# Stick-breaking heads: q and k projected with stationary weights, a GpSimd product for the second chunk, and idle projection tiles lent as extra buffers

## The chip, the core and the metric

The kernel runs as one program on one core of a Trainium2 chip. The core has a matrix engine (TensorE, PE in the profile; its weight loads are the row PEld), a vector engine (VectorE, DVE), a scalar engine (ScalarE, ACT), a general-purpose engine (GpSimd, POOL), a queue engine (SyncE, SP) that issues most of the transfers, and 16 DMA engines that carry them out. Each engine works through its own queue in order and waits on semaphores for the others. The metric is the device time of one execution in microseconds, lower is better. Numbers that are compared are medians of several executions; the profile is of one execution.

## The reference

The reference is one layer of a residual block over 2048 positions of width 1024, in float32. What matters here is the stick-breaking half of the attention:

```python
u = rms_norm(x, norm1_w)
proj = u @ w_in                       # -> diff q, k, v | sb q, sk, sv
# 4 differential-attention heads on the first half, then 8 stick-breaking heads of width 64:
z = einsum('bqhd,bkhd->bhqk', qb, k) * 64 ** -0.5
mask = k_pos < q_pos
log_1mb = where(mask, log_sigmoid(-z), 0)
rem = cumsum(log_1mb, reverse=True) - log_1mb
a = where(mask, exp(log_sigmoid(z) + rem), 0)
out = einsum('bhqk,bkhd->bqhd', a, v)
# then: h = x + concat(y_diff, rms_norm(y_sb)) @ w_out ; h = h + SwiGLU(rms_norm(h))
```

For each query row, every earlier key gets a weight beta = sigmoid(z) times the product of (1 - beta) over the keys between it and the query. The kernel forms that product directly with a scan over sigmoid(-z), from the last key to the first.

## The kernel before

Almost every matrix product is taken in split float16: a float32 number is held as a high half and a low half, and a product is the sum of three float16 products (high by high, high by low, low by high) accumulated in PSUM. So most tensors exist as a pair of halves, and "split" in the code means making that pair.

The attention runs over eight groups g. Groups 0 to 3 are the four differential heads; groups 4 to 7 are two stick-breaking heads each (index m = 0, 1 within the group). For each group there is a projection (`proj`, 16 row tiles t of 128 positions) and an attention part (`diff_attn` for g < 4, `sb_attn` for the others). The projections run ahead of the attention: `advance` emits tiles of group g + 1 while group g attends, so matrix work of the projection lies among the attention's. The order in each engine's queue is set by a scheduler when the program is built, from the order of emission, the priorities in `PRI` and its own model of times; `note` and `pick` keep a running account of the load of ACT, DVE and POOL, and choose an engine for operations that may go to more than one.

A projection tile before (`proj_tile`, line 320) loads a 128 by 128 piece of the normalised input as the stationary operand and streams 384 columns of the weights past it (128 for q, 128 for k, 128 for v): 24 matmuls of 384 columns for one tile, into one PSUM tile `pj`. There are two such PSUM tiles (`psj`, two buffers). `proj_out` then splits v, and for g >= 4 splits q and k into the staging tile `st` (lines 327 and 330). Positions lie on the partitions there, but the scores need the head dimension on the partitions, so after every four tiles `proj_batch` turns `st` with two transposing transfers into `qT` and `kT` (line 372), and two more transfers copy the halves of `qT` with their partition halves exchanged (line 374). In `kT` each head m has its 64 high rows and its 64 low rows stacked on the 128 partitions; with `qT` stacked the same way and with the exchanged copy, two matmuls give all four products of halves.

One step of `sb_attn` is `stage_a(i, m, b)`: query tile i, head m, key block b of up to 1024 keys, done in chunks of up to 512 keys, from the last chunk (c = 1 where the block has more than 512 keys) to the first (c = 0). For a chunk, `score_chunk` (line 448) puts scores into one of four PSUM tiles `sc`; ACT writes sigmoid(-z) into the SBUF tile `om` (line 554) and sigmoid(z) over the scores in PSUM (line 555); DVE runs the reversed product scan over `om` (line 557) and multiplies the two into `be` (line 558). Where a query tile has two key blocks, the first column of one block's `om` is copied to the next (line 547). When the block is whole, `split_t` makes the high half of `be` on ACT (line 89) and the low half on POOL (line 98) in a tile `s16` (three buffers), and one transposing transfer, issued by SP, turns both into `aT` (line 403, six buffers). `stage_b` multiplies `aT` with v (`pv`, line 458). Up to PD = 5 steps wait between the two stages. The tiles `z4` for `be` and `om` have nine buffers.

Group 7 has no projection after it; instead the output projection of the finished rows (`out_proj`, line 761) is placed beside it. The projection's pool (`pp`) also holds the tiles `st` and `raw`, two buffers each. `raw` is used by the projections of g < 4, and `st` by all; in group 7 `raw` takes a part of the output weights and `st` the residual rows. After the attention comes the SwiGLU part, which the change does not touch.

Of the kernel before, what the change touches and what calls it, by code (L numbers as in the profile page):

```python
# [11 lines left out]
F32 = mybir.dt.float32  # L12
# [18 lines left out]
NG = 8  # L31
# [28 lines left out]
def block(tc, a, out):  # L60
# [3 lines left out]
    with top:  # L64
# [62 lines left out]
        DVE.memset(mhalf[:], -0.5)  # L127

# [122 lines left out]
        with ExitStack() as ph1:  # L251
# [71 lines left out]

            def split_psum(hi, lo, src, n):
# [8 lines left out]
            @pri("po")  # L333
            def proj_out(g, G, pj, B, j):
                st, v, raw = B
                nv = 1 if g < 4 else 2
                vv = v[:, j, :].rearrange("p (h s e) -> p h s e", h=nv, s=2)
                split_psum(vv[:, :, 0, :], vv[:, :, 1, :], pj[:, 256:384].rearrange("p (h e) -> p h e", h=nv), 128)
                if g < 4:
                    if pick(A=270, D=335) == "A":  # L340
                        ACT.mul(raw[:, j, :], pj[:, :256], 2.0 ** -11)
                    else:
                        DVE.tensor_scalar(raw[:, j, :], pj[:, :256], 2.0 ** -11, None, op0=ALU.mult)
                else:
                    split_psum(st[:, 0:4, j, 0, :], st[:, 0:4, j, 1, :], pj[:, :256].rearrange("p (c e) -> p c e", c=4), 256)

            @pri("pb")
            def proj_batch(g, G, B):
                st, v, raw = B
                qT = sp.tile([P, 4, 4, P], F16, tag="qT", bufs=QB, name=nm("qT"))  # L350
                kT = sp.tile([P, 2, 4, P], F16, tag="kT", bufs=KB, name=nm("kT"))
                if g < 4:
                    rq = raw[:].rearrange("p t (c e) -> p t c e", e=64)
                    sq = st[:].rearrange("p c t s e -> p (c t s e)")[:, :2048].bitcast(F32)
                    ACT.activation(sq.rearrange("p (t c e) -> p t c e", t=4, c=4), rq, AF.Square)
                    note("A", 950)
                    ss = sm.tile([P, 16], F32, tag="ss", bufs=2, name=nm("ss"))
                    DVE.tensor_reduce(ss[:], sq.rearrange("p (c e) -> p c e", e=64), op=ALU.add, axis=AX.X)
                    rs = sm.tile([P, 16], F32, tag="rs", bufs=2, name=nm("rs"))
                    rstd(rs[:], ss[:], 2.0 ** -16 / 64, G["epsk"][:])  # L360
                    rsb = rs[:].rearrange("p (t c) -> p t c", c=4).unsqueeze(3).to_broadcast([P, 4, 4, 64])
                    DVE.tensor_tensor(rq, rq, rsb, ALU.mult)
                    note("D", 2300)
                    gb = gk[:].unsqueeze(1).unsqueeze(1).to_broadcast([P, 4, 2, 64])
                    tt(rq[:, :, 2:4, :], rq[:, :, 2:4, :], gb, ALU.mult, 512)
                    for o in range(2):
                        src = rq[:, :, 2 * o : 2 * o + 2, :]
                        d = st[:, 2 * o : 2 * o + 2].rearrange("p c t s e -> p t c s e")
                        to16(d[:, :, :, 0, :], src, 512)
                        tt(d[:, :, :, 1, :], src, d[:, :, :, 0, :], ALU.subtract, 512)  # L370
# [8 lines left out]
            def proj(g, G, fresh=None):  # L379
                for t in range(NT):  # L380
# [6 lines left out]
                    if t % 4 == 0:  # L387
                        st = pp.tile([P, 4, 4, 2, 64], F16, tag="st", name=nm("st"))
                        v = sp.tile([P, 4, 256], F16, tag="v", bufs=KB, name=nm("v"))
                        raw = pp.tile([P, 4, 256], F32, tag="raw", name=nm("raw")) if g < 4 else None  # L390
# [145 lines left out]
            def sb_attn(g, G):  # L536
# [691 lines left out]
```

## Time and profile before

| | us |
|---|---|
| median of three runs (lowest, highest) | 2735.74 (2730.43, 2737.0) |
| the profiled execution | 2740.3 |
| its span from first to last instruction | 2738.5 |
| busy in the span: PE / DVE / POOL / ACT | 2490.0 / 1978.5 / 1429.8 / 1353.3 |
| first and last start of the stick-breaking sigmoid (line 554) | 605.4 and 1378.7 |

A row of the profile's groups reads: line, engine, operation, written tile <- read tiles, shape, count, then busy time in us, mean duration in ns, and the idle time of the engine just before these instructions with what ended it. The matmul durations overlap, because matmuls are pipelined; their rate is read from the starts of consecutive runs in the timeline. The granted clock of PE is a share of full speed.

### The profile page before, as it was taken

The page shows a single profiled execution, that of the slowest core. Times are in us where ns is not written, and L with a number is a line of the kernel's source. Part 1 is how long each engine was busy: PE and PEld are TensorE (multiplying, and loading weights), DVE is VectorE, ACT ScalarE, POOL GpSimd, SP SyncE. Part 2 cuts the span into 40 slices and gives each one's busy share as a digit, 9 for nine tenths or more (in the row PEclk, how much of TensorE's full clock was granted, in tenths as well). Part 3 has the DMA queues.
Part 4 walks back from the last instruction along what each step waited for, and adds up shares of the span by engine and source line. Part 5 has one row for each costly group of instructions (what it writes and reads, how often), then busy time and mean ns, then how long its engine had stood idle before and what let it go on. Part 6 is the DMA issues. An engine that isn't in the chain of part 4 may idle for free.

```text
span 2738.5 us, 45414 instructions
## 1 busy us (share of the span) xinstructions
PE 2490.0 (91%) x17084; PEld 1409.8 (51%) x17084; DVE 1978.5 (72%) x3752; ACT 1353.3 (49%) x2539; POOL 1429.8 (52%) x1002
## 2 busy tenths in 40 slices
PE   7998989898978886889989898999999999999999
PEld 4655656565545553457775444444444444444444
DVE  6888879888888989987766777777786544434434
ACT  4665656566868778765644534344342212121121
POOL 2577677765554545546655566565664332222322
PEclk9999999998999997899999999999999999999999
DMA  6788787789998997997896665566657845635532
GB/s 227 199 164 178 151 198 164 180 171 200 208 201 184 212 186 151 203 192 208 213 289 256 220 234 191 208 221 216 231 204 283 316 158 181 220 128 193 192 116 93
DMA packets 646830, 543.52 MB, mean 198 GB/s; under 512 B 506369, under 2 KB 573953, under 8 KB 636369
## 3 DMA queue, kind: packets, MB, share of 16 engines
q1 hardware_dynamic: 644784, 538.53, 71.8%
q8 instruction: 134, 2.20, 0.3%
q0 software_dynamic: 512, 1.36, 0.2%
q10 hardware_dynamic: 1312, 0.72, 0.1%
q14 instruction: 88, 0.71, 0.1%
HBM read 261.08 MB, written 147.32 MB: 149 GB/s over the span
## 4 chain that ended last, share of the span: by engine, by line
PE 36%; DVE 9%; DMA 4%; POOL 3%; issue 3%; ACT 2%; SPq 0%; DVEq 0%; POOLq 0%; ACTq 0%
PE pd L1034 14%; PE pm L934 7%; PE pd L934 5%; PE pa L934 5%; DVE wd L215 2%; PE po L761 2%; DMA stages<-in_w_down_dram 1%; POOL stages L98 1%; DVE wu L215 1%; DMA aT<-s 1%; DVE z L557 1%; DVE cg L999 1%; DVE cg L98 1%; POOL s L98 1%; PE pj L320 1%
## 5 line engine op out<-in xcount | busy, mean ns | idle before, releaser
L98 POOL TENSOR_TENSOR s<-z,s 128x1024 f16<-128x1024 f32 (+7 forms) x288 | 474.4, 1655 | 320.1 <-ACT s L89 281.4
L320 PE MATMUL pj<-w,xt 128*128 128x384 f16 x3072 | 577.0, 336 | 19.2 <-DMA xt<-xs 5.6
L320 PEld LDWEIGHTS <-xt 128*128 128x128 f16 x3072 | 301.5, 101 | 233.1 <-issue 36.1
L557 DVE TENSOR_TENSOR_SCAN z<-z,sc 128x512 f32<-128x512 f32 (+3 forms) x320 | 356.1, 1114 | 72.1 <-ACT sc L555 68.8
L448 PE MATMUL sc<-kT,qT 128*128 128x512 f16 (+3 forms) x1280 | 348.3, 364 | 59.4 <-DVE z L558 23.7
L1034 PE MATMUL pd<-wd,act 128*128 128x512 f16 x1764 | 394.0, 381 | 7.2 <-DVE cu L968 7.1
L458 PE MATMUL yp<-v,aT 128*128 128x64 f16 (+1 forms) x4896 | 281.5, 209 | 82.3 <-DMA aT<-s 81.7
L458 PEld LDWEIGHTS <-aT 128*128 128x128 f16 x4896 | 245.4, 102 | 172.1 <-DMA aT<-s 110.4
L934 PEld LDWEIGHTS <-wg 128*128 128x128 f16 x1848 | 181.8, 98 | 228.1 <-issue 14.6
L934 PEld LDWEIGHTS <-wu 128*128 128x128 f16 x1848 | 180.8, 98 | 216.5 <-issue 2.0
L98 POOL TENSOR_TENSOR act<-cg,act 128x512 f16<-128x512 f32 x109 | 149.8, 1385 | 262.3 <-ACT act L993 262.3
L1034 PEld LDWEIGHTS <-act 128*128 128x128 f16 x1764 | 173.0, 98 | 216.6 <-issue 10.2
L89 ACT CAST s<-z 128x128 f16<-128x128 f32 (+7 forms) x216 | 170.3, 790 | 154.8 <-DMA aT<-s 72.9
L98 POOL TENSOR_TENSOR stages<-stages 128x512 f32<-128x512 f32 x97 | 172.9, 1783 | 120.1 <-DVE wg L215 41.4
L98 POOL TENSOR_TENSOR hs<-hs,cu 128x512 f32<-128x512 f32 x102 | 132.6, 1306 | 165.6 <-DVE hs L1040 62.7
L554 ACT ACTIVATE z<-sc,c 128x512 f32<-128x512 f32 (+3 forms) x320 | 204.4, 639 | 23.7 <-PE sc L448 18.9
L558 DVE TENSOR_TENSOR z<-sc,z 128x512 f32<-128x512 f32 (+3 forms) x320 | 193.7, 606 | 8.5
L555 ACT ACTIVATE sc<-sc,c 128x512 f32<-128x512 f32 (+3 forms) x320 | 196.5, 614 | 0.0
L1040 DVE SCALAR_TENSOR_TENSOR hs<-pd,c,hs 128x512 f32<-128x512 f32 x144 | 106.5, 748 | 118.5 <-PE pd L1034 113.6
L761 PE MATMUL po<-wo,mt 128*128 128x256 f16 x1536 | 180.7, 275 | 12.3 <-DVE xf L764 6.8
L993 ACT CAST act<-cg 128x512 f16<-128x512 f32 x126 | 76.9, 616 | 231.4 <-DVE cg L999 192.7
L934 PE MATMUL pm<-X,wu 128*128 128x512 f16 x792 | 179.1, 379 | 1.8 <-ACT cg L979 1.7
(241 smaller groups left out, 4109.1 us busy)
## 6 DMA issues: line engine op xcount, KB each, us to landing
xt<-xs SPq DMA_DIRECT2D x112, 512.0 KB, 4.4
hs<-hd SPq DMA_DIRECT2D x72, 512.0 KB, 4.5
hd<-hs SPq DMA_DIRECT2D x56, 512.0 KB, 5.8
split<-wg SPq DMA_DIRECT2D x11, 1792.0 KB, 6.9
split<-wu SPq DMA_DIRECT2D x11, 1792.0 KB, 6.7
split<-wd SPq DMA_DIRECT2D x11, 1792.0 KB, 6.8
wg<-split SPq DMA_DIRECT2D x11, 1792.0 KB, 7.4
wd<-split SPq DMA_DIRECT2D x11, 1792.0 KB, 9.1
```

What stands on the lines that cost most here:

```text
L89: ACT.copy(dst, src)
L98: (DVE if e == "D" else POOL).tensor_tensor(dst, a_, b_, op)
L320: PE.matmul(pj[:, :384], lhsT=xv[:, xi, kt, :], rhs=G["w"][:, wi, kt, :], start=n == 0, stop=n == 23)
L448: PE.matmul(sc[:, : 128 * w].rearrange("p (t n) -> p t n", n=P), lhsT=G["q"][i // 4][:, 2 - 2 * o + m, i % 4, :], rhs=G["k"][q][:, m, 0:w, ...
L458: PE.matmul(yp[:, y0 : y0 + wd], lhsT=aT[:, a_, :], rhs=v[:, v_ : v_ + wd], start=start and j == 0 and q == 0, stop=stop and j == nb - 1 a ...
L554: ACT.activation(om[:, lo:hi], sc[:, :w], AF.Sigmoid, scale=G["nkz"][:])
L555: ACT.activation(sc[:, :w], sc[:, :w], AF.Sigmoid, scale=G["kz"][:])
L557: DVE.tensor_tensor_scan(ov, ov, sc[:, :w], om[:, hi : hi + 1], op0=ALU.mult, op1=ALU.bypass)
L558: DVE.tensor_tensor(be[:, lo:hi], sc[:, :w], om[:, lo + 1 : hi + 1], ALU.mult)
L761: PE.matmul(po[:, sl], lhsT=mt[:, kt, P * xi : P * xi + P], rhs=wos[2 * h + n][wi][:, kt, :], start=q == 0, stop=q == 23)
L934: PE.matmul(ps_[:].rearrange("p (t n) -> p t n", n=P), lhsT=wv[:, wo, wi, 128 * kt : 128 * kt + 128], rhs=X[xo][:, :, xi, kt, :], start=st ...
L1034: PE.matmul(po[:], lhsT=act[:, ao, xi, 128 * j : 128 * j + 128], rhs=W["d"][:, wo, wi, :], start=start and u == 0 and q == 0, stop=u == nu ...
```

## The change

Four things change, all in the stick-breaking groups 4 to 7.

First, q and k are projected the other way round. `proj_turned` takes a 128 by 128 piece of the weights as the stationary operand and streams the 128 positions of the input past it, so that q and k come out with the head dimension on the partitions. Only v keeps the old orientation. A tile is now 72 matmuls of 128 columns in the place of 24 of 384. Two tiles share a pair of PSUM tiles, `pq` (q and k) and `pv` (v), which together are both buffers of `psj`. `turned_out` reads them once for the pair: q is written for each head with the other head's 64 rows multiplied by zero (the constant `half`), as a high part on ACT and a low part on DVE; k and v are split as before. The two transposing transfers and the two exchange copies for every four tiles are gone in these groups.

Second, a score chunk is three matmuls in the place of two: masked high q by high k, masked low q by high k, masked high q by low k.

Third, for the chunk c = 1 ACT writes sigmoid(z) into `be` in SBUF, and the product with the scan moves from DVE to POOL. The chunk c = 0 stays on DVE.

Fourth, in groups 4 to 6 `split_t` takes its `s16` tile from the two idle `raw` tiles in two of five steps, and its `aT` tile from the two idle `st` tiles in one of four, and 7 steps in the place of 5 may wait between the stages. Group 7 keeps the old numbers.

```diff
+        half = c1(2, "half")
+        DVE.memset(half[:], 0.0)
+        for m in range(2):
+            DVE.memset(half[64 * m : 64 * m + 64, m : m + 1], 2.0 ** -11)
...
+            @pri("pm")
+            def proj_turned(G, xt, pq, pv, r):
+                xv = xt[:].rearrange("p (s k n) -> p s k n", s=2, k=KT)
+                for c in range(3):
+                    n = 0
+                    for kt in range(KT):
+                        for xi, wi in ((0, 0), (0, 1), (1, 0)):
+                            w_, x_ = G["w"][:, wi, kt, 128 * c : 128 * c + 128], xv[:, xi, kt, :]
+                            o = pv[:, P * r : P * r + P] if c == 2 else pq[:, 256 * c + P * r : 256 * c + P * r + P]
+                            PE.matmul(o, lhsT=x_ if c == 2 else w_, rhs=w_ if c == 2 else x_, start=n == 0, stop=n == 23)
+                            n += 1
+
+            @pri("po")
+            def turned_out(pq, pv, qT, kT, v, j):
+                two = slice(j - 1, j + 1)
+                q2, k2 = (pq[:, 256 * c : 256 * c + 256].rearrange("p (t n) -> p t n", t=2) for c in range(2))
+                for m in range(2):
+                    ACT.mul(qT[:, m, two, :], q2, half[:, m : m + 1])
+                    DVE.scalar_tensor_tensor(qT[:, 2 + m, two, :], q2, half[:, m : m + 1], qT[:, m, two, :], op0=ALU.mult, op1=ALU.subtract)
+                note("A", 800)
+                note("D", 800)
+                split_psum(kT[:, 0, two, :], kT[:, 1, two, :], k2, 256)
+                vv = v[:, two, :].rearrange("p t (h s e) -> p t h s e", h=2, s=2)
+                split_psum(vv[:, :, :, 0, :], vv[:, :, :, 1, :], pv[:, :256].rearrange("p (t h e) -> p t h e", t=2, h=2), 256)
...
-                else:
-                    split_psum(st[:, 0:4, j, 0, :], st[:, 0:4, j, 1, :], pj[:, :256].rearrange("p (c e) -> p c e", c=4), 256)
...
+                    if g >= 4:
+                        if t % 4 == 0:
+                            qT, kT = new_qk()
+                            G["q"].append(qT)
+                            G["k"].append(kT)
+                            G["v"].append(v)
+                        if t % 2 == 0:
+                            pq, pv_ = (psj.tile([P, 512], F32, tag="pj", name=nm("pj")) for _ in range(2))
+                        proj_turned(G, xt, pq, pv_, t % 2)
+                        if t % 2 == 1:
+                            turned_out(pq, pv_, qT, kT, v, t % 4)
+                        yield
+                        continue
...
-            def split_t(src, n, he="ADP", le="DP"):
-                s16 = s16p.tile([P, 2048], F16, tag="s16", bufs=SB, name=nm("s16"))
+            def split_t(src, n, he="ADP", le="DP", wide=None):
+                if wide is not None and wide % 5 in (1, 3):
+                    s16 = pp.tile([P, 4, 256], F32, tag="raw", name=nm("s16"))[:].rearrange("p t n -> p (t n)").bitcast(F16)
+                else:
+                    s16 = s16p.tile([P, 2048], F16, tag="s16", bufs=SB, name=nm("s16"))
...
-                aT = sp.tile([P, 16, P], F16, tag="aT", bufs=AB, name=nm("aT"))
+                if wide is not None and wide % 4 == 3:
+                    aT = pp.tile([P, 4, 4, 2, 64], F16, tag="st", name=nm("aT"))[:].rearrange("p c t s e -> p (c t) (s e)")
+                else:
+                    aT = sp.tile([P, 16, P], F16, tag="aT", bufs=AB, name=nm("aT"))
...
-            def score_chunk(G, sc, i, q, m, w, cut=False):
-                for o in range(2):
-                    PE.matmul(sc[:, : 128 * w].rearrange("p (t n) -> p t n", n=P), lhsT=G["q"][i // 4][:, 2 - 2 * o + m, i % 4, :], rhs=G["k"][q][:, m, 0:w, :], start=o == 0, stop=o == 1)
+            def score_chunk(G, sc, i, q, m, w, cut=False, turned=False):
+                terms = ((m, 0), (2 + m, 0), (m, 1)) if turned else ((2 + m, m), (m, m))
+                for o, (a_, b_) in enumerate(terms):
+                    PE.matmul(sc[:, : 128 * w].rearrange("p (t n) -> p t n", n=P), lhsT=G["q"][i // 4][:, a_, i % 4, :], rhs=G["k"][q][:, b_, 0:w, :], start=o == 0, stop=o == len(terms) - 1)
...
+                lag = PD + 2 if g < NG - 1 else PD
...
-                        ACT.activation(sc[:, :w], sc[:, :w], AF.Sigmoid, scale=G["kz"][:])
+                        ACT.activation(beta, sc[:, :w], AF.Sigmoid, scale=G["kz"][:])
...
-                        DVE.tensor_tensor(be[:, lo:hi], sc[:, :w], om[:, lo + 1 : hi + 1], ALU.mult)
+                        (POOL if aside else DVE).tensor_tensor(be[:, lo:hi], beta, om[:, lo + 1 : hi + 1], ALU.mult)
...
-                            if len(pend) > PD:
+                            if len(pend) > lag:
```

Here `aside` is `c == 1`, and `beta` is the slice of `be` for that chunk and the score tile `sc` otherwise. The code that differential heads alone use stands in `proj_batch` as before.

More of the change, by code (lines that the diff above doesn't have):

```diff
@@ L349, in proj_batch @@
                 st, v, raw = B
[L350 to L365, printed above, removed]
-                    for o in range(2):
[L367 to L370, printed above, removed]
@@ new lines, in proj_batch @@
+                qT, kT = new_qk()
+                rq = raw[:].rearrange("p t (c e) -> p t c e", e=64)
+                sq = st[:].rearrange("p c t s e -> p (c t s e)")[:, :2048].bitcast(F32)
+                ACT.activation(sq.rearrange("p (t c e) -> p t c e", t=4, c=4), rq, AF.Square)
+                note("A", 950)
+                ss = sm.tile([P, 16], F32, tag="ss", bufs=2, name=nm("ss"))
+                DVE.tensor_reduce(ss[:], sq.rearrange("p (c e) -> p c e", e=64), op=ALU.add, axis=AX.X)
```

46 lines of the change are left out of this document (33 added, 13 removed).

## The prediction

> **What bounds the kernel now.** I read the page first, for the engines' shares over the span:
>
> ```profile
> PE 2490.0 (91%) x17084; PEld 1409.8 (51%) x17084; DVE 1978.5 (72%) x3752; ACT 1353.3 (49%) x2539; POOL 1429.8 (52%) x1002
> ```
>
> A mean of 91% on PE says PE, but it mixes stages. The change touches only the stick-breaking groups, so I cut that stretch into the four groups (where the steps of one give way to the next's) and asked for busy time in each:
>
> ```profile
> core 0: us, PE busy (x) PEld busy (x) DVE busy (x) ACT busy (x) POOL busy (x), PEclk, DMA share, GB/s
> 606.00:797.00 191.00, 164.97 (x1617) 104.31 (x1615) 168.28 (x315) 147.98 (x290) 103.19 (x64) 0.94 1.02 205
> 797.00:968.00 171.00, 139.04 (x1420) 86.41 (x1418) 151.35 (x267) 133.39 (x252) 87.56 (x55) 0.91 0.99 196
> 968.00:1125.00 157.00, 120.52 (x1255) 73.77 (x1256) 145.79 (x242) 128.61 (x240) 79.72 (x53) 0.85 0.86 171
> 1125.00:1400.00 275.00, 239.83 (x2498) 186.31 (x2496) 209.80 (x357) 175.12 (x325) 161.36 (x113) 0.96 0.87 207
> ```
>
> The rows are groups 4, 5, 6 and 7. In group 6 DVE is the fullest (145.8 of 157, 93%); in group 5 it leads PE by 12 us; in group 4 PE and DVE are level; in group 7, with the output projection beside it, PE leads (87%). No engine is full, so there are waits. The table of waits over 605 to 1385 us says which:
>
> ```profile
> POOL s L98 <- ACT s L89: 273.0, 122, 7.2
> DVE z L557 <- ACT sc L555: 68.8, 65, 5.6
> PE yp L458 <- DMA aT<-s: 54.6, 50, 2.9
> ACT s L89 <- DMA aT<-s: 52.0, 38, 3.9
> PE sc L448 <- DVE z L558: 23.7, 27, 2.4
> ```
>
> Each row is total us, times, longest. Two matter: PE waits 54.6 us for a turned tile to land, and ACT waits 52.0 us for a transposing transfer to give back an `s16` tile. POOL's 273 us is slack. So I take three groups as set by DVE together with the wait on transposes, and the last by PE.
>
> **The projection (first edit).** PE streams the same columns. The rate is read from starts:
>
> ```profile
> 703.31 2.76 PE L320 MATMUL pj<-w,xt 128*128 128x384 f16 x16
> 705.91 0.59 PE L448 MATMUL sc<-kT,qT 128*128 128x512 f16 x2
> 706.34 1.30 PE L320 MATMUL pj<-w,xt 128*128 128x384 f16 x7
> ...
> 434.52 0.94 PE L458 MATMUL yp<-v,aT 128*128 128x128 f16 x14
> 435.30 0.59 PE L448 MATMUL sc<-kT,qT 128*128 128x512 f16 x2
> ```
>
> Sixteen of 384 columns take 705.91 - 703.31 = 2.60 us, 162.5 ns each; two of 512 take 0.43 us, 215 ns each; fourteen of 128 columns, each with its own weight load, take 0.78 us, 56 ns each. Three of 128 are 168 ns for 162.5: 64 tiles x 24 x 5.5 ns = 8 us more over all groups, a quarter each. It cannot be a gain, since no column goes away; the bound above is these 8 us, as long as the weight loads stay hidden as they do in the row of 128.
>
> The output of a pair of tiles, from these rows:
>
> ```profile
> L330 DVE SCALAR_TENSOR_TENSOR st<-pj,st 128x256 f16<-128x256 f32 x58 | 23.4, 407 | 2.9 <-ACT st L327 2.9
> L327 ACT ACTIVATE st<-pj 128x256 f16<-128x256 f32 x58 | 22.6, 395 | 13.7 <-DVE v L330 13.4 <-PE sc L450 0.3
> L327 ACT ACTIVATE v<-pj 128x128 f16<-128x128 f32 x57 | 16.5, 296 | 2.7 <-PE pj L320 2.6
> L330 DVE SCALAR_TENSOR_TENSOR v<-pj,v 128x128 f16<-128x128 f32 x58 | 15.7, 275 | 3.0 <-ACT v L327 2.9
> ```
>
> Before, DVE: 2 x (407 + 275) = 1364 ns; after, four of 407 = 1628. ACT: 1382 before, 1580 after. Over 32 pairs DVE pays 8.4 us and ACT 6.3 us, some 2 us a group each. What is new is that a pair holds both PSUM tiles, so the next pair's q cannot start until this pair's q and k are read: four DVE and up to four ACT operations, some 2 us. PE's queue is in order, so a stall there holds up scores behind it. I cost it at nothing, because a pair is needed only every 20 us or so and scores and `pv` matmuls lie between; if that cover goes it is at most 32 x 2 = 64 us.
>
> The transfers that go:
>
> ```profile
> L372 SPq DMA_TRANSPOSE qT<-st x32: 1232/1266/2467, 71.7 to 1207.6; - x32
> L372 SPq DMA_TRANSPOSE kT<-st x32: 1231/1325/3494, 73.8 to 1208.9; - x32
> L374 SPq DMA_DIRECT2D qT<-qT x64: 467/586/1172, 75.8 to 1216.8; - x64
> L403 SPq DMA_TRANSPOSE aT<-s x288: 1167/1782/6046, 113.9 to 1388.4; - x144
> ```
>
> Half of lines 372 and 374 belongs to these groups: SP's queue loses 16 x (1.27 + 1.33) + 32 x 0.59 = 60 us of issuing, all ahead of some `aT`. In columns, 16 x 2 x 1024 = 32,768 go and 2 x 1088 x 128 = 278,528 of `aT` stay: a tenth fewer. I book this with the waits below, not by itself.
>
> **The third score matmul (second edit).** One matmul more for each chunk. The chunks by width are in the rows of the next fence (224 of 512, 32 each of 384, 256, 128): 224 x 215 + 32 x (162 + 109 + 56) ns = 58.6 us (109 for 256 columns lies midway between 162 and 56) at full clock, 14.6 a group. No gain is possible from it; it is all on PE.
>
> **The GpSimd product (third edit).** Of the chunks, c = 1 are 80 of 512 columns and 16 each of 384, 256 and 128 (query tiles 4 to 15 in the first key block, 12 to 15 in the second, 8 heads). DVE's price, and POOL's nearest rows:
>
> ```profile
> L558 DVE TENSOR_TENSOR z<-sc,z 128x512 f32<-128x512 f32 x224 | 153.6, 686 | 5.2
> L558 DVE TENSOR_TENSOR z<-sc,z 128x384 f32<-128x384 f32 x32 | 17.7, 554 | 1.2
> L558 DVE TENSOR_TENSOR z<-sc,z 128x256 f32<-128x256 f32 x32 | 13.4, 420 | 1.0
> L558 DVE TENSOR_TENSOR z<-sc,z 128x128 f32<-128x128 f32 x32 | 9.2, 289 | 1.0
> L98 POOL TENSOR_TENSOR s<-z,s 128x512 f16<-128x512 f32 x16 | 18.5, 1156 | 15.9 <-ACT s L89 15.8
> L98 POOL TENSOR_TENSOR z<-z,z 128x512 f32<-128x512 f32 x7 | 9.9, 1418 | 3.6 <-DVE z L98 3.3
> ```
>
> DVE loses 80 x 686 + 16 x (554 + 420 + 289) ns = 75 us, 18.8 a group. POOL gains, per 512 columns, between 1156 ns (half the bytes in one input) and 1418 ns (all float32); I take 1.3 us because the operands are float32 and this stage has little DVE traffic with two SBUF inputs: about 135 us, 34 a group, which its 273 us of waiting covers. ACT's write to SBUF in place of PSUM is within the spread of lines 554 and 555. The scan of c = 0 runs on DVE meanwhile (1.3 us and then its product), so the later product of c = 1 is mostly hidden; if not, it is 128 x 0.6 = 77 us of delay in a chain that has seven steps of slack.
>
> **The buffers (fourth edit).** Five `s16` tiles for three and eight `aT` for six in groups 4 to 6, with two more steps between the stages. That is aimed at the two DMA waits quoted. I take most of it away in these three groups; group 7 keeps its numbers. What is late next is the busiest engine.
>
> **The sum.** PE's work at full clock is busy time times granted clock (an estimate), plus 14.6 and 2:
> group 4: PE 165.0 x 0.94 + 16.6 = 172, DVE 168.3 - 18.8 + 2 = 151, ACT 150, POOL 137;
> group 5: PE 143, DVE 135, ACT 135, POOL 122;
> group 6: PE 119, DVE 129, ACT 130, POOL 114;
> group 7: PE 247 of 275, DVE 193.
> Now the fullest engine fills 88 to 93% of a stretch. I take 93% where one engine leads (group 4: 172 / 0.93 = 185, 6 us less) and 90% where three lie close (group 5: 143 / 0.9 = 159, 12 less; group 6: 130 / 0.9 = 144, 13 less). Group 7 pays its PE work, 16.6 less 9, half of DVE's 18.8, since DVE ends waits of PE there only now and then: 8 more. Sum: -6 - 12 - 13 + 8 = -23 us. The profiled execution took 2740.3 us (span 2738.5), 4.6 above the median of three, 2735.74; from the median the forecast is **2713 us**.
>
> The Trainium skill (TensorE: Matmul & The Clock Gate, "What's actually happening") says that the array runs at half or at full clock by how busy it has lately been. The rows above agree: clock 0.85 where PE is busy 77% of the stretch, 0.91 at 81%, 0.94 at 86%. By that rule the added matmuls would partly pay for themselves, which is the second rival.
>
> **The rivals.**
> (a) Slower: PE becomes the bound in every group, because its waits only move. What speaks for it: PE is already the fullest engine in group 7, level in group 4, and gets 66.6 us of work. What speaks against it: 94.5 us of PE idle in groups 4 to 6 (26 + 32 + 36.5), most of it behind DVE and transposes. If the idle of groups 5 and 6 takes their share but groups 4 and 7 pay theirs in full, the time is 2735.7 + 2 x 16.6 = 2769. It decides once PE's waits in groups 4 to 6 stay above some 70 us.
> (b) The clock is granted whole: with PE denser, group 6's 0.85 and group 5's 0.91 rise to group 7's 0.96 and the waits on transposes vanish. Then all three fill to 95%: 181, 151, 137 and group 7 even: -50 us, 2686.
> (c) No change: POOL's product comes late, `be` and its split with it, and what DVE gives is waited away: 77 us of delay against 75 us given, 2736. For it: POOL would take both the product and the split of one step, 1.3 + 2.2 us, in one queue. Against it: POOL ends at 71 to 73% busy (137 of 191, 122 of 171, 114 of 157).
>
> **How the numbers follow.** Forecast 0.48, (b) 0.20, (c) 0.10, (a) 0.22. A measurement here tells a change from none at about 0.3%, 8 us. The forecast and (b) are faster; (c) is within; (a) is slower, with a little of the forecast's spread shared out: faster 0.67, same 0.10, slower 0.23. The likeliest case alone spans 2698 to 2726 (fill one or two points either way). The range takes in (b) and half of the way to (a): 2684 to 2755.
>
> **What the profile after would show.** Line 558's product: 75 us less on DVE and 128 new products on POOL of 1.2 to 1.4 us per 512 columns. Scores: 960 matmuls in these groups, 59 us more of PE at full clock. No transposes into `qT` or `kT` after group 3. The waits of PE and ACT for `aT` falling from 107 us to some 40. Group 6 near 144 us, group 7 near 283. The prediction is wrong if PE shows new waits before the projection's matmuls on the reads of a pair, if POOL's product exceeds 1.5 us, or if the granted clock does not rise.

## The result and the profile after

The changed kernel is slower: median 2748.71 us (2741.3 to 2764.68) against 2736.37 us (2730.28 to 2741.37) of the kernel before on the same chip. The ratio is 1.0059 with a 95% interval of 1.0039 to 1.0079. The forecast was 2713 us, faster. Below, a difference between two kernels is taken from their ratios; 0.1% is 2.7 us. The profiled execution took 2753.49 us, its span is 2751.7 us, 13.2 more than before.

The page's first part, busy time of each engine over the whole span:

```profile
PE 2524.5 (92%) x20476; PEld 1544.2 (56%) x20476; DVE 1958.6 (71%) x3686; ACT 1355.5 (49%) x2494; POOL 1525.8 (55%) x1116
```

DVE gives up only 20 us here, for 75 us of products taken from it. The four groups after, cut as those before, a like distance behind the last carried column of the group (columns: stretch, its length, busy time of PE, PEld, DVE, ACT, POOL with counts, granted clock, DMA share, GB/s):

```profile
core 0: us, PE busy (x) PEld busy (x) DVE busy (x) ACT busy (x) POOL busy (x), PEclk, DMA share, GB/s
606.00:775.00 169.00, 145.47 (x2242) 117.61 (x2240) 148.03 (x256) 138.95 (x259) 125.21 (x94) 0.98 0.85 173
775.00:943.00 168.00, 145.14 (x2258) 117.61 (x2257) 142.99 (x250) 135.07 (x244) 114.67 (x88) 0.97 0.91 175
943.00:1109.00 166.00, 142.08 (x2140) 113.82 (x2138) 141.04 (x240) 129.34 (x233) 111.79 (x86) 0.94 0.89 172
1109.00:1412.00 303.00, 261.80 (x3207) 221.23 (x3204) 218.60 (x355) 177.97 (x320) 177.40 (x132) 0.98 0.77 186
```

Groups 4 to 7 take 169, 168, 166 and 303 us where 185, 159, 144 and 283 were forecast (191, 171, 157 and 275 before). The first three together are 16 us shorter, the last is 28 us longer. The stretches don't hold the same work, though: by the counts of projection matmuls in them (24 a tile before, 72 after) they hold 22.5, 16.2, 10.0 and 8.1 tiles of the projection before, and 15.6, 15.7, 14.8 and 11.7 after. So the first stretch is shorter mainly because projection work was put off to later ones. Busy time times clock, an estimate, gives 142.6 + 140.8 + 133.6 + 256.6 = 673.6 us of PE work at full clock, against 155.1 + 126.5 + 102.4 + 230.2 = 614.2 before: 59.4 more, 66.4 forecast; with clocks of two digits, that is equal within a few us. So the size of PE's load was nearly right; how much of it would vanish into idle time was not.

The cuts follow the attention. The projection, which runs ahead of it, can be followed by the starts of its matmuls and of those behind it (line, count, durations, first and last start). Before, and then after:

```profile
L320 PE MATMUL pj<-w,xt x3072: 322/326/528, 25.9 to 1200.2; 128*128 128x384 f16 x192
L761 PE MATMUL po<-wo,mt x1536: 269/273/421, 1205.6 to 1457.6; 128*128 128x256 f16 x192
```

```profile
L338 PE MATMUL pj<-xt,w x3072: 216/219/314, 535.2 to 1221.0; 128*128 128x128 f16 x192
L817 PE MATMUL po<-wo,mt x1536: 269/273/421, 1230.5 to 1475.3; 128*128 128x256 f16 x192
L990 PEld LDWEIGHTS <-wg x1848: 95/98/152, 1475.3 to 2676.3; 128*128 128x128 f16 x185
```

The last matmul of the projection of q and k starts 21 us later, the output projection begins 25 us later and ends 18 us later (1457.6 to 1475.3). Before, the feed-forward part began at 1457.6 too, and lasted 2738.5 - 1457.6 = 1280.9 us; after, 2751.7 - 1475.3 = 1276.4. So the attention ran 16 us ahead of its former self through group 6 while the projections fell back, and group 7, where the output projection has to wait for the last projection (the program puts it behind the projection, and it uses the same PSUM tiles), paid for it. In all 17 profiles of this case, the experiments below included, the output projection begins 3 to 13 us after the last projection matmul and ends 239 to 265 us after it, while that last matmul itself comes anywhere between 1174 us (e1) and 1298 us (e11). Most of what the edits do to the time is thus done to the moment at which the projections are through.

How full PE is up to there (from the first sigmoid to the last projection, and to the feed-forward part), before:

```profile
606.00:1200.00 594.00, 485.60 (x4862) 301.71 (x4860) 526.70 (x951) 462.16 (x898) 306.72 (x199) 0.90 0.96 194
606.00:1457.00 851.00, 715.58 (x7234) 495.60 (x7232) 705.40 (x1230) 602.38 (x1124) 458.84 (x300) 0.93 0.93 208
```

and after:

```profile
606.00:1221.00 615.00, 524.39 (x8022) 426.40 (x8020) 519.25 (x915) 480.19 (x887) 416.24 (x320) 0.96 0.87 174
606.00:1475.00 869.00, 750.26 (x10325) 618.84 (x10323) 682.70 (x1155) 599.99 (x1075) 553.94 (x414) 0.97 0.85 190
```

PE fills 82% of its first stretch before and 85% after, with 485.6 x 0.90 = 437 and 524.4 x 0.96 = 503 us of work at full clock. Of these 66 us more, the higher clock took back, by the same estimate, some 27 (busy time rose by 39 only) and PE's idle some 18 (from 108 to 91 us); the other 21 are the later end of the projection. The forecast wanted the fullest engine at 90 to 93%. What PE and ACT wait for, after (total us, times, longest):

```profile
POOL z L612 <- DVE z L611: 123.1, 71, 7.3
POOL s L98 <- ACT s L89: 95.6, 74, 5.6
PE yp L508 <- DMA aT<-s: 69.9, 54, 5.1
ACT z L608 <- PE sc L498: 41.5, 30, 5.2
ACT s L89 <- DMA aT<-s: 23.1, 20, 2.8
```

The buffers did what they do for ACT: its wait for a transposing transfer falls from 52.0 to 23.1 us. But PE's wait for a turned tile rises from 54.6 to 69.9. In groups 4 to 6 alone, which have the extra buffers, ACT's falls from 44.0 to 14.3 us and PE's rises from 44.3 to 57.0. POOL has a new wait of 123 us, for the scan whose product it now makes.

### The profile page after: what moved, and what is told of

Its sections match the earlier page's. It is cut to its first block, busy times and chain, and to the rows that moved or that the text cites. A ratio compares the mean times of both kernels' runs of the same rounds, so it can differ in the third digit from the quotient of the medians.

```text
span 2751.7 us, 52232 instructions
## 1 busy us (share of the span) xinstructions
PE 2524.5 (92%) x20476; PEld 1544.2 (56%) x20476; DVE 1958.6 (71%) x3686; ACT 1355.5 (49%) x2494; POOL 1525.8 (55%) x1116
## 4 chain that ended last, share of the span: by engine, by line
PE 40%; DVE 11%; DMA 9%; POOL 6%; issue 5%; ACT 4%; SPq 0%; DVEq 0%; POOLq 0%; ACTq 0%
PE pd L1090 13%; PE pm L990 8%; PE pd L990 6%; PE pa L990 5%; DMA aT<-s 5%; DVE z L611 3%; POOL s L98 3%; PE po L817 2%; PE pj L338 2%; PE sc L498 2%; DVE wd L220 2%; DMA stages<-in_w_down_dram 1%; POOL stages L98 1%; POOL z L612 1%; PE yp L508 1%
## 5 line engine op out<-in xcount | busy, mean ns | idle before, releaser
L498 PE MATMUL sc<-kT,qT 128*128 128x512 f16 (+3 forms) x1600 | 397.9, 354 | 20.5 <-DVE z L533 3.5
L508 PE MATMUL yp<-v,aT 128*128 128x64 f16 (+1 forms) x4896 | 290.6, 205 | 97.7 <-DMA aT<-s 95.1
L325 PE MATMUL pj<-w,xt 128*128 128x384 f16 x1536 | 287.5, 334 | 11.7 <-ACT raw L369 5.8
L338 PE MATMUL pj<-xt,w 128*128 128x128 f16 x3072 | 249.1, 225 | 9.6 <-DVE v L360 6.4
L338 PEld LDWEIGHTS <-w 128*128 128x128 f16 x3072 | 214.5, 101 | 29.4 <-issue 9.6
L325 PEld LDWEIGHTS <-xt 128*128 128x128 f16 x1536 | 151.3, 100 | 118.0 <-issue 19.4
L612 POOL TENSOR_TENSOR z<-z,z 128x512 f32<-128x512 f32 (+3 forms) x128 | 121.7, 952 | 133.2 <-DVE z L611 123.1
```

Source lines behind the costliest of these rows:

```text
L325: PE.matmul(pj[:, :384], lhsT=xv[:, xi, kt, :], rhs=G["w"][:, wi, kt, :], start=n == 0, stop=n == 23)
L338: PE.matmul(o, lhsT=x_ if c == 2 else w_, rhs=w_ if c == 2 else x_, start=n == 0, stop=n == 23)
L498: PE.matmul(sc[:, : 128 * w].rearrange("p (t n) -> p t n", n=P), lhsT=G["q"][i // 4][:, a_, i % 4, :], rhs=G["k"][q][:, b_, 0:w, :], start ...
L508: PE.matmul(yp[:, y0 : y0 + wd], lhsT=aT[:, a_, :], rhs=v[:, v_ : v_ + wd], start=start and j == 0 and q == 0, stop=stop and j == nb - 1 a ...
L612: (POOL if aside else DVE).tensor_tensor(be[:, lo:hi], beta, om[:, lo + 1 : hi + 1], ALU.mult)
```

## The experiments

The theory after the result: the added PE work sets the time, because PE's waits were not taken away. The rivals: the turned projection costs more than its PE work (the reads, the pair that holds both PSUM tiles); the GpSimd product or the extra buffers do harm.

### The score matmuls: one fewer, one more

```diff
-                terms = ((m, 0), (2 + m, 0), (m, 1)) if turned else ((2 + m, m), (m, m))
+                terms = ((m, 0), (2 + m, 0)) if turned else ((2 + m, m), (m, m))                        # e1
+                terms = ((m, 0), (2 + m, 0), (m, 1), (2 + m, 1)) if turned else ((2 + m, m), (m, m))    # e2
```

> The changed kernel with the third score matmul (high q by low k) left out, so a part of the scores' precision is missing; PE loses the 58.6 us that the change added for scores and is else the same. Theory P (PE's added work sets the time, 60 us of it against 43 us of recovered idle): 25 to 45 us less than the changed kernel, a ratio to before of 0.990 to 0.997. Theory Q (POOL's product stands ahead of the split of the step before in POOL's queue, the transposes come late and PE waits for them): PE only waits longer, under 10 us less, ratio 1.002 to 1.006.

> The changed kernel with a fourth score matmul (low q by low k): PE gets another 58.6 us. Theory P: 30 to 50 us more than the changed kernel, ratio to before 1.017 to 1.024. Theory Q: PE has waits to put it into, under 15 us more, ratio under 1.012.

With two, 2706.93 us, ratio 0.9906 (0.9889 to 0.9923). With four, 2780.28 us, ratio 1.0174 (1.0153 to 1.0196). So the third matmul costs 1.53%, 42 us of its 58.6, and a fourth 1.15%, 31 us. Without the third the change is a gain of 26 us, at the price of high q by low k, which is then missing from the scores. The same stretches with two terms, to its last projection and its feed-forward part:

```profile
606.00:1170.00 564.00, 471.82 (x7622) 399.39 (x7620) 506.31 (x896) 461.98 (x862) 408.11 (x310) 0.95 0.93 187
606.00:1421.00 815.00, 696.96 (x9999) 592.61 (x9997) 681.36 (x1155) 594.01 (x1071) 556.24 (x412) 0.96 0.90 202
```

and with four:

```profile
606.00:1250.00 644.00, 572.15 (x8309) 448.33 (x8307) 528.55 (x918) 481.44 (x888) 421.76 (x320) 0.97 0.82 167
606.00:1507.00 901.00, 807.35 (x10637) 645.11 (x10635) 688.90 (x1155) 599.77 (x1074) 555.60 (x413) 0.97 0.80 184
```

To the feed-forward part they take 815, 869 and 901 us with two, three and four: 54 and 32 more. The third matmul is paid nearly in full there (in these single profiles 8 us of the 54 come back later, where nothing differs). PE fills 84, 85 and 89% of the first stretch, and its idle time there is 92, 91 and 72 us: the third matmul took nothing from it. Work on PE is thus not hidden, though PE is idle for a seventh of the time. The fourth looks cheaper, but 42 and 31 us are not apart by these intervals. In its one profile some of it falls into the wait for turned tiles, which is 42.9 us with four:

```profile
PE yp L508 <- DMA aT<-s: 42.9, 42, 4.2
```

### The product back on DVE, the buffers away, and both

```diff
-                        aside = c == 1
+                        aside = False                                  # e3, e6
-                lag = PD + 2 if g < NG - 1 else PD
+                lag = PD                                               # e4, e6
-                    return n, split_t(be[:, :n], n, "A", "P", wide[0] if g < NG - 1 else None)
+                    return n, split_t(be[:, :n], n, "A", "P", None)    # e4, e6
```

> The changed kernel with the product of the second chunk back on DVE; turned projection, three score matmuls and extra buffers stay. Theory Q: the waits of PE on aT fall from 70 us to 40 or less and the time falls by 10 us or more, ratio 1.002 or less. Theory P: DVE gets its 75 us back in groups where it was the fullest, 5 to 25 us more than the changed kernel, ratio 1.008 to 1.015.

> The changed kernel with three s16 tiles, six aT tiles and five waiting steps in every group, as before. If the extra buffers do what the prediction booked for them: ACT's waits for aT go back from 23 us to some 50 and the time rises by 10 to 20 us, ratio 1.009 to 1.013. If the transposes are late for another reason (Q), the time moves by less than 8 us either way, ratio 1.003 to 1.009.

> The changed kernel with edits one and two alone: turned projection and three score matmuls; the product on DVE and the old buffers. Theory P: PE's 66 us against the 60 us of SP and a tenth of the transposes: slower than the changed kernel by about what e3 showed, ratio 1.008 to 1.014. If the turned projection with its lighter transposes is a gain, 1.000 to 1.005.

Product on DVE: 2757.52 us, 1.0095 (1.0079 to 1.0110). No buffers: 2744.42 us, 1.0045 (1.0031 to 1.0060). Neither, that is the first two edits alone: 2763.85 us, 1.0115 (1.0093 to 1.0136). The product on POOL is worth some 10 us in the changed kernel. The buffers are worth nothing that these intervals show, perhaps 4 us the wrong way, where 10 to 20 us were expected if they did what the prediction booked. So neither does the harm: the 31 us of the first two edits are the loss, and the other two win back 15. But both make PE wait for turned tiles. Its wait with neither (e6), with buffers alone (e3) and with the product alone (e4):

```profile
PE yp L508 <- DMA aT<-s: 38.1, 29, 4.1
```

```profile
PE yp L508 <- DMA aT<-s: 46.1, 41, 4.3
```

```profile
PE yp L508 <- DMA aT<-s: 49.4, 44, 3.7
```

With both it is 69.9. Why is argued, not shown: POOL works through its queue in order, the next step's product stands there ahead of the last step's split, and the product waits 123 us in all for a scan, so splits and with them transposes start late. A kernel with the split first wasn't tried. Nor is this wait the loss itself: e3 takes the product off POOL, shortens PE's wait by 24 us, and is 10 us slower.

### The turned projection with two matmuls and nothing else

```diff
-                terms = ((m, 0), (2 + m, 0), (m, 1)) if turned else ((2 + m, m), (m, m))
+                terms = ((m, 0), (2 + m, 0)) if turned else ((2 + m, m), (m, m))
...
-                        aside = c == 1
+                        aside = False
```

The lines of the buffers are undone as in e6.

> The turned projection alone with two score matmuls (high q by low k left out, so a part of the scores' precision is missing), the product on DVE and the old buffers: what turning the projection is worth without the third matmul. From e1 and the changed kernel the third matmul costs some 42 us; e6 stands 31 us over before. If the price of the matmul is the same here, 8 to 14 us less than before, ratio 0.994 to 0.998. If it is smaller where DVE is the fuller engine (75 us of product back on it), the matmul is worth 15 to 30 us here and the ratio is 1.001 to 1.006.

2745.86 us, ratio 1.0059 (1.0042 to 1.0077). With the product on DVE and the old buffers, the turned projection itself is a loss of 16 us, though its transfers are gone. Its waits:

```profile
PEld L508 <- DMA aT<-s: 62.8, 53, 4.5
PE yp L508 <- DMA aT<-s: 49.2, 39, 4.3
PE sc L498 <- DVE z L612: 31.5, 37, 2.0
ACT s L89 <- DMA aT<-s: 27.7, 16, 4.9
```

ACT's wait for transposes is halved (52.0 to 27.7), which fits the 60 us of issuing taken from SP's queue, but PE waits longer for DVE's product (31.5 against 23.7), and DVE is busy 716.8 us up to the feed-forward part, 11 more than before. So DVE, with the reads of the turned tiles on it, seems to be in the way; this is read from waits and busy times, and no run takes these reads off DVE. With e1, e6 and the changed kernel this closes a square:

| | product on DVE, old buffers | product on POOL, extra buffers |
|---|---|---|
| two score matmuls | 1.0059 (e12) | 0.9906 (e1) |
| three score matmuls | 1.0115 (e6) | 1.0059 (after) |

The last two edits are worth 42 us with two matmuls and 15 with three; the third matmul costs 15 us where DVE is full and 42 where it isn't. The parts don't add: relieving DVE makes PE's work the price, and PE's work eats what DVE gave.

### The product on POOL in the kernel before

The two differences behind `aside` and the notes are those of the change (e5); e7 adds the two `raw` tiles for `s16`, without longer `lag` or `aT`.

```diff
-                        ACT.activation(sc[:, :w], sc[:, :w], AF.Sigmoid, scale=G["kz"][:])
+                        aside = c == 1
+                        beta = be[:, lo:hi] if aside else sc[:, :w]
+                        ACT.activation(beta, sc[:, :w], AF.Sigmoid, scale=G["kz"][:])
...
-                        DVE.tensor_tensor(be[:, lo:hi], sc[:, :w], om[:, lo + 1 : hi + 1], ALU.mult)
+                        (POOL if aside else DVE).tensor_tensor(be[:, lo:hi], beta, om[:, lo + 1 : hi + 1], ALU.mult)
...
+                if wide is not None and wide % 5 in (1, 3):            # e7
+                    s16 = pp.tile([P, 4, 256], F32, tag="raw", name=nm("s16"))[:].rearrange("p t n -> p (t n)").bitcast(F16)
```

> The kernel before with the third edit alone: the product of the second chunk on POOL, sigmoid(z) of that chunk written to SBUF; old projection, two score matmuls, old buffers. Theory P (PE's added work cost the time, the POOL product is a gain): 10 to 35 us less than before, ratio 0.987 to 0.996, since DVE loses 75 us in groups 5 and 6 where it is the fullest and PE gets nothing. If the POOL product is only worth something beside the other edits, ratio 0.997 to 1.003.

> The kernel before with the POOL product and with the two idle raw tiles as extra s16 tiles in groups 4 to 6 (st is in use by the old projection, so aT stays at six; five waiting steps). If extra s16 tiles are worth what the prediction took (ACT waits 52 us for them before): 5 to 15 us less than the POOL product alone. If not, within 5 us of it.

e5: 2724.35 us, ratio 0.9971 (0.9959 to 0.9982). e7: 2722.11 us, 0.9967 (0.9954 to 0.9979). A gain, but of 8 to 9 us for 75 us off DVE, less than the 10 to 35 expected of e5; and e7's two tiles add 1 us where 5 to 15 were expected. What took its place in e5:

```profile
ACT s L89 <- DMA aT<-s: 71.4, 50, 3.6
PE yp L458 <- DMA aT<-s: 56.1, 59, 1.9
```

ACT's wait for transposes rises from 52.0 to 71.4 us. In e7 that wait is 23.9 us, and PE's is 77.8: the wait moves along the chain from ACT to PE, as it did in the changed kernel. Against e7, e1 (with a turned projection, two matmuls, and more buffers still) is 17 us faster: beside the product on POOL the turned projection seems to gain, as long as the third matmul is left out.

### How the turned tiles are read

e8 puts q, k and v of one tile into one PSUM tile and reads them tile by tile, so a pair no longer holds both. e9 keeps the pair but writes q and k in stacked halves (high rows of a head on its own 64 partitions, low rows on the others), so that two matmuls give all four products, with two SP copies for every four tiles; e10 is e9 without the extra buffers, e11 is e10 tile by tile.

```diff
-                            o = pv[:, P * r : P * r + P] if c == 2 else pq[:, 256 * c + P * r : 256 * c + P * r + P]
+                            o = pq[:, P * c : P * c + P]               # e8, e11
...
+                for T, o, src in ((qT, 2, q2), (kT, 0, k2)):           # e9, e10, e11
+                    for m in range(2):
+                        hi, lo = slice(64 * m, 64 * m + 64), slice(64 - 64 * m, 128 - 64 * m)
+                        ACT.mul(T[hi, o + m, two, :], src[hi], 2.0 ** -11)
+                        DVE.scalar_tensor_tensor(T[lo, o + m, two, :], src[hi], 2.0 ** -11, T[hi, o + m, two, :], op0=ALU.mult, op1=ALU.subtract)
+                if j == 3:
+                    for o in (0, 64):
+                        SP.dma_start(qT[o : o + 64, 0:2].rearrange("p c t n -> p (c t n)"), qT[64 - o : 128 - o, 2:4].rearrange("p c t n -> p (c t n)"))
...
-                terms = ((m, 0), (2 + m, 0), (m, 1)) if turned else ((2 + m, m), (m, m))
+                terms = ((2 + m, m), (m, m))                           # e9, e10, e11
```

> The changed kernel with the turned projection put out tile by tile: q, k and v of one tile in one PSUM tile, so that the other is free for the next, in the place of a pair that holds both. If holding both PSUM tiles stalls PE: 8 us or more less than the changed kernel. If PE's added work is all of it: within 5 us, or up to 10 us more for twice as many reading operations of half the width.

> The changed kernel with the two score matmuls of the kernel before: the turned projection writes for each head the high rows on the head's own 64 partitions and the low rows on the other 64, and two copies exchange the halves of qT for every four tiles; no transposing transfers, POOL product and extra buffers stay. PE loses the 58.6 us, ACT and DVE get one more half-height operation each a pair, some 14 us in all. Theory P: faster than before and near the run with a matmul left out, ratio 0.989 to 0.996. If the reads of PSUM that write to other partitions are the new bound (DVE): ratio 0.996 to 1.003.

> The same as e9_stacked with three s16, six aT and five waiting steps in every group. If the extra buffers are worth anything when PE is not the bound: 4 us or more slower than e9_stacked. If they are worth nothing, as e4 showed beside three matmuls: within 4 us of it or faster.

> The same as e10_stacked_no_bufs with the projection put out tile by tile, so that a tile holds one of the two PSUM tiles in the place of a pair that holds both. Twice as many operations of half the width: ACT and DVE pay some 25 us each more. If they are slack: within 4 us. If holding both tiles costs: faster by 4 us or more. If DVE is the bound: slower by 5 to 15 us.

e8: 2743.94 us, 1.0046 (1.0030 to 1.0062), which overlaps the changed kernel's interval: holding both tiles costs nothing that can be told. e9: 2736.02 us, 1.0022 (1.0012 to 1.0031), 10 us better than the change, yet 1.16% (32 us) behind the two matmuls of e1 and outside the 0.989 to 0.996 that the theory of PE's added work expected: something in the stacked form takes back most of what the third matmul cost. e10: 2748.41 us, 1.0055 (1.0043 to 1.0068), so there the buffers are worth 9 us. e11: 2822.68 us, 1.0331 (1.0317 to 1.0345), by far the worst, and 75 us behind e10 where at most 15 were expected. Its reads of q in the stretch from 606 to 1260 us:

```profile
L349 DVE SCALAR_TENSOR_TENSOR qT<-pj,qT 64x128 f16<-64x128 f32 x111 | 31.8, 288 | 22.4 <-ACT qT L348 19.4
L348 ACT ACTIVATE qT<-pj 64x128 f16<-64x128 f32 x111 | 30.0, 273 | 42.9 <-PE pj L338 26.2 <-DVE qT L349 15.5
```

On half the partitions an operation costs about as much as on all (273 and 288 ns, against 296 on ACT and 275 on DVE for 128 rows of 128 columns in the kernel before), so splitting by head and by tile doubles the count twice, and each DVE operation waits for ACT's and the next of ACT's for DVE's. Neither half does it alone: e8, tile by tile in full height, loses nothing, and e10, in half height by pairs, is 75 us faster. Busy time doesn't explain it either: over the whole projection DVE's reads of q and k take 73 us against 54 in e10, but the last projection matmul comes at 1298 us against 1215. That the waits between ACT and DVE are the cause is argued, not shown, and so is that e9 loses its 32 us to e1 in the same way.

### The account of the engines' load

The change books less load on DVE, and the scheduler's `pick` sends it other work. e13 puts the former note back in the changed kernel, e14 in e9, e15 in e7.

```diff
-                        note("D", 2.1 * w + 150)
-                        note("P" if aside else "D", (1.65 if aside else 1.05) * w + 100)
+                        note("D", 3.15 * w + 350)
```

> The changed kernel with the account of engine loads as before the change (3.15 ns an element and 350 ns a chunk on DVE, nothing on POOL), so that the high halves of k and v go to ACT and most of the output rows' operations to POOL; the product stays on POOL. If the work sent back to DVE ate the gain: DVE 25 to 40 us less busy and 8 us or more less than the changed kernel, ratio 1.003 or less. If PE alone sets the time: DVE less busy and the time within 5 us of the changed kernel, ratio 1.004 to 1.008.

> e9_stacked (turned projection, two full score products, POOL product, extra buffers) with the old account. If DVE is its bound: 8 us or more less than e9_stacked, ratio 0.990 to 0.999. If the reading of the turned tiles by ACT and DVE in turn is: within 5 us of it, ratio 1.000 to 1.004.

> e7_pool_raw (kernel before, POOL product, two extra s16 tiles) with the old account. There are no turned tiles here, so only few operations move: within 5 us of e7_pool_raw, ratio 0.994 to 0.999; more than 8 us less if the output rows' operations on DVE held it up.

e13: 2737.25 us, 1.0027 (1.0016 to 1.0039), 9 us better than the change. Its stretch to the feed-forward part:

```profile
606.00:1462.00 856.00, 747.08 (x10334) 617.62 (x10332) 654.41 (x1095) 607.69 (x1117) 567.98 (x427) 0.97 0.84 192
```

DVE does 28 us less there than after (682.7). In these profiles the last projection matmul comes at the same time in both (1223 us); e13's gain lies behind it, in the output projection, which ends 239 us after it in place of 252. e14: 2746.25 us, 1.0062 (1.0048 to 1.0077), the wrong way by 0.4% and outside both expectations; why stays open. e15: 2715.14 us, 0.9949 (0.9937 to 0.9961), the fastest full kernel here, 14 us faster than before and 30 faster than the change (its intervals and e7's overlap, so the account's own share is not shown). It has the former projection and two score matmuls, the product on POOL, two more `s16` tiles and the old account. PE waits 80.7 us for turned tiles in it, longer than in the changed kernel: such a total says little by itself about the time.

## Why the prediction was wrong, step by step

**The step that failed** is the fourth edit's "I take most of it away in these three groups", and the fill of 90 to 93% that the sum builds on it. The waits of PE and ACT for `aT`, which were to fall from 107 us to some 40, came out at 69.9 + 23.1 = 93: ACT's fell, PE's rose, and PE stayed at 86% busy in groups 4 to 6. Taking the buffers away changes nothing that can be told (e4), and in the kernel before they add 1 us (e7). Where PE's idle doesn't give way, work that is added to PE is paid, and e1 shows it: the third matmul costs 42 of its 58.6 us, with PE's idle at 92 us without it and 91 with it.

In the terms of the sum, groups 4 to 6 gave 16 us for the 31 forecast, and group 7 cost 28 us for 8. The sum also left each group its old share of the projection, but 3.6 tiles more than before were left for group 7. And it set PE's work at full clock against the stretch, as if the clock were whole; at 0.98, 0.97 and 0.94 PE was busy 3, 4 and 9 us longer than that.

What came is nearest to the prediction's rival (a), "its waits only move": PE's idle in groups 4 to 6 came out at 23.5 + 22.9 + 23.9 = 70 us, just where (a) was to decide. It didn't come as (a) was posed, with groups 4 and 7 paying in full, and (a) gave +33 us where the change costs 16. That the first two edits alone cost 31 us (e6), near (a)'s 33, is luck: e12 puts half of it down to the turned projection, which the prediction counted at 2 us a group.

**DVE's relief was mis-sized.** The sum took 18.8 - 2 us a group, 67 in all; to the feed-forward part DVE fell by 705.4 - 682.7 = 22.7. The product itself left as priced (193.7 to 117.7 us). Rows of after for the product and for the reads:

```profile
L612 DVE TENSOR_TENSOR z<-sc,z 128x512 f32<-128x512 f32 x144 | 98.2, 682 | 3.4
L612 POOL TENSOR_TENSOR z<-z,z 128x512 f32<-128x512 f32 x80 | 90.2, 1128 | 80.6 <-DVE z L611 74.8 <-DVE z L597 5.1 <-DVE c L175 0.6
L346 ACT ACTIVATE qT<-pj,half 128x256 f16<-128x256 f32 x64 | 31.8, 497 | 28.0 <-PE pj L338 16.3 <-DVE qT L347 11.7
L347 DVE SCALAR_TENSOR_TENSOR qT<-pj,half,qT 128x256 f16<-128x256 f32 x64 | 30.0, 469 | 5.8 <-ACT qT L346 5.8
L357 ACT ACTIVATE v<-pj 128x256 f16<-128x256 f32 x13 | 5.5, 424 | 1.1 <-PE pj L338 1.1
L360 DVE SCALAR_TENSOR_TENSOR kT<-pj,kT 128x256 f16<-128x256 f32 x32 | 13.2, 413 | 0.7 <-ACT kT L357 0.4
L359 DVE TENSOR_SCALAR kT<-pj 128x256 f16<-128x256 f32 x27 | 11.1, 412 | 0.0
L359 DVE TENSOR_SCALAR v<-pj 128x256 f16<-128x256 f32 x19 | 7.9, 414 | 7.7 <-PE pj L338 7.7
```

The account, told that DVE had room, sent it 46 of the 64 high halves of k and v (19 us) that the prediction had on ACT, and some 17 us more of the output rows' arithmetic (line 98); the reads of q and the low halves of k and v take 12 us more than the reads before. The masked reads of q take 497 ns on ACT and 469 on DVE, not 395 and 407 as priced from rows of the same shape. Unmasked reads of that shape in the same kernel take 424 on ACT, and the same operation on DVE takes 413 without the mask, so the mask costs 73 ns on ACT and 56 on DVE. In e6, e12 and e13, where ACT makes nearly all such reads, it costs 75 to 87.

The Trainium skill (ScalarE: Activation LUTs, "What ACT_TABLE_LOAD costs") says that each per-partition pointer operand adds about 93 ns to an ACTIVATE. The difference here is 73 ns within the kernel and 497 - 395 = 102 against the row that the prediction used, so the trace agrees about as to size, and the prediction should have priced it.

**The projection was right**: PE's added work came out at 59 us for 66, no transposes into `qT` or `kT` are left in these groups (the last starts at 560.9 us), and PE's stall on the reads of a pair stayed small:

```profile
L338 PE MATMUL pj<-xt,w 128*128 128x128 f16 x3072 | 249.1, 225 | 9.6 <-DVE v L360 6.4 <-DVE m L183 2.8 <-DVE z L597 0.4
```

9.6 us of idle, against the 64 named as the most it could cost; e8 says the same. What the prediction did not see is that the first edit loses when it stands alone with two matmuls (e12, +16 us). It counted the reads as 2 us a group; they fall on the engine that was fullest, which fits the loss but isn't tested by itself.

**The product on POOL was right in size** (1.13 us per 512 columns, forecast 1.2 to 1.4), so rival (c), a late product that gives nothing, is out as posed: e3 and e5 show gains of 10 and 8 us. But it isn't worth what the sum took either: in e5 the waits of ACT at the transposes grow by 19 us, as what DVE gives is waited for elsewhere.

**The clock did rise**, as rival (b) assumed: 0.94, 0.91, 0.85 and 0.96 became 0.98, 0.97, 0.94 and 0.98. It did not bring (b)'s time, since the fill didn't follow. The Trainium skill (TensorE: Matmul & The Clock Gate, "What's actually happening") ties the clock to how busy the array has lately been. The rows agree in group 6: 0.85 at 77% busy before, 0.94 at 86% after. They also show that the share of a whole stretch doesn't fix the clock, since at 86% it is 0.94 in group 4 before and 0.98, 0.97 and 0.94 in groups 4 to 6 after.

**The range held the time** (2684 to 2755) only by its reach towards (a), a slower kernel; what it was built around was faster. None of the three signs that were to show the prediction wrong came either: the pair's reads stall PE by 9.6 us, POOL's product stays under 1.5 us, and the clock rose. They watched other places than the one that failed. Afterwards the chance of a slower kernel, 0.23, looks small: two edits of four put work on an engine that led or was level in two groups, and the gain hung on one untested sentence about waits.

## What to carry to other kernels

Idle time on an engine isn't room for more work on it as long as the wait behind it stays: here PE was idle 15% of the stretch and still paid 42 of 58.6 us for a third matmul. Price an edit that relieves one engine together with the edit that loads another, since their worths don't add (15 or 42 us for the same pair), and try the relief alone first: POOL's product gains 8 us in the old kernel by itself. An edit's worth can even change its sign with what stands beside it: turning the projection, with two matmuls, loses 16 us when DVE is full (e12) and is 17 us faster than the old projection when POOL has the product and there are more buffers (e1 against e7). In the masked form the third matmul, which the full product needs, takes that gain away. When an operation moves between engines, look at what a load account then sends to the engine that was relieved.

## What was not expected of the hardware

Masking 64 of 128 rows by a per-partition factor made the reads of PSUM dearer on both engines, by 73 ns on ACT and 56 on DVE for 256 columns. In e8, with 128 columns, they take 396 against 276 to 284 ns on ACT and 336 against 285 on DVE, so the addition doesn't shrink with the width. POOL's float32 product of 512 columns took 1128 ns, about as much as its split from float32 and float16 to float16 in the kernel before (1156), though it reads more bytes. And four reads of half the partitions, tile by tile, cost the kernel 2.8% over the same reads by pairs (e11 against e10), the largest effect of any run here.
